# Expert lists ranked downwards by the first key, taken from the ninth block on, and built in bfloat16

## The chip, the cores and the metric

The program runs on one core of one Trainium2 chip. The metric is device time in microseconds of one execution. The five engines of the core are named as in the profile: PE (TensorE, with PEld for its weight loads), DVE (VectorE), ACT (ScalarE), POOL (GpSimd) and SP (which only issues transfers here). Each engine runs its instructions in the order of the program; semaphores make one wait for another.

## What is computed

Two transformer blocks over 256 tokens of width 2048. The change touches the first block's attention, its expert layer, and the second block's latent attention. The expert layer, cut from the reference:

```python
def peer(x, w_pq, sub_k1, sub_k2, u_emb, v_emb):      # 8 heads, 128 keys in each half, top 16
    q = (xt @ w_pq).reshape(T, PEER_HEADS, 2, PEER_HALF)
    s1 = jnp.einsum('thd,hkd->thk', q[:, :, 0], sub_k1, ...)
    s2 = jnp.einsum('thd,hkd->thk', q[:, :, 1], sub_k2, ...)
    v1, i1 = lax.top_k(s1, PEER_TOPK)
    v2, i2 = lax.top_k(s2, PEER_TOPK)
    cand = (v1[..., :, None] + v2[..., None, :]).reshape(T, PEER_HEADS, PEER_TOPK * PEER_TOPK)
    cidx = (i1[..., :, None] * N_KEYS + i2[..., None, :]).reshape(...)
    sc, sel = lax.top_k(cand, PEER_TOPK)
    eidx = jnp.take_along_axis(cidx, sel, axis=-1)
    gates = jax.nn.softmax(sc, axis=-1)
    ...
        act = jax.nn.gelu(jnp.einsum('cd,ced->ce', xc, u_emb[ic]))
        return jnp.einsum('ce,ced->cd', (gc * act).astype(...), v_emb[ic])
```

The first block's attention has 16 heads of width 64 in four groups that share a key head. The latent attention adds two products for a score: one over 128 columns of the head, and one over 64 rotary columns whose key is shared by all heads.

## The kernel before

**Arithmetic.** Every large product is a sum of three fp32r products of halves (`mm3`, lines 133 to 136): a weight tile `raw` of 128x2048 arrives by DMA, ACT rounds each half of it to `whi` (L123), DVE takes the rest as `wlo` (L124), and PE multiplies 12 times 512 columns for each half. `whi` and `wlo` have four buffers each, so DVE and ACT run at most four halves ahead of PE.

**The expert layer.** All 16384 rows of `u_emb` are multiplied (the u phase): 32 chunks of 512 experts, which is four values of key 1 each, in the order of key 1. A chunk is 8 halves, 8 transposes of the activations, and two DMAs into a table `AG` in DRAM, whose row is (key 1 + 1) x 128 + key 2. Beside it, DVE, ACT and a little of PE work out the routing at a lower priority: the top 16 (`top16`), the gate tables (`gsb`, which SP writes into `AG` in four pieces, with a maximum `um` over each, L679), and then the lists. A list says which experts are used: list A by both token tiles (42 blocks of 128 places), list B by the first tile alone (29), list C by the second alone (30). The order of an expert in its list is its rank, counted upwards in key 1 by a scan over `colsum` (L715).

**The lists.** Each of 16 steps (L742 to L753, J = 8) builds on DVE a one-hot `ln` of the lane (L744), a one-hot `b1` of the block (L746) and a product `bb` (L750); ACT builds the other half of `bb` (L749). PE then adds eight products of `ln` and `bb` into one PSUM bank (L753). `ids`, `idv` and `idg` (L755 to L763) are the finished lists. `ln`, `b1` and `bb` have two buffers each.

**The v phase.** For each block of a list, POOL gathers 128 rows of `v_emb` (`raw` or `vraw`, by `idv`) and the rows of `AG` for two or four blocks at once (`vag`, by `idg`). `gated` multiplies activation and gate into `vh` (L827), splits it into `vhh` and `vhl`, and PE adds 12 or 24 products into eight PSUM banks `acc`. POOL, DVE, ACT and PE take all this in the order in which a scheduler put it when the program was built; the schedule holds for all engines.

**Attention.** `attn1` (first block) makes the scores of two heads on partitions 0 to 63 of `qT` and `kT`, then of two on 64 to 127 (L444), and `softmax_out` multiplies the transposed weights `pT` with the values (L429): heads 0 and 1 into output partitions 0 to 63, heads 2 and 3 into 64 to 127. The latent attention (L1110, L1111) alternates a product over 128 partitions with one over 64. A fp32 matmul of the program is two MATMUL instructions in the trace.

Of the kernel before, what the change touches and what calls it, by code (L numbers as in the profile page):

```python
# [18 lines left out]
ALU = mybir.AluOpType  # L19
# [37 lines left out]
def tile_kernel(ctx: ExitStack, tc: tile.TileContext, A, out):  # L57
# [355 lines left out]
    def softmax_out(s, l, nh, vget, oget):  # L413
# [3 lines left out]
        for h in range(nh):  # L417
            V.tensor_scalar(s[:, h, :], s[:, h, :], r[:, h:h + 1], None, op0=ALU.mult)
        for h in range(0, nh, 2):
# [6 lines left out]
            S.activation(pT, tp.rearrange("p (a t) -> p a t", a=4), AF.Copy)  # L426
            for hh in range(2):
# [7 lines left out]
    def attn1(c, f, tt, qT):  # L435
# [4 lines left out]
        for e in range(2):  # L440
            ps = bank("sc")
            b = slice(e * 64, e * 64 + 64)
            for j in range(2):
                TE.matmul(ps[:, j * T:(j + 1) * T], lhsT=qT[b, 2 * f + j, tt * P:(tt + 1) * P],  # L444
                          rhs=kT[b, g, :], start=True, stop=True)
            V.tensor_tensor(s[:, 2 * e:2 * e + 2, :], ps.rearrange("p (a t) -> p a t", a=2),
                            maskb[:, tt, :].unsqueeze(1).to_broadcast([P, 2, T]), op=ALU.add)
# [6 lines left out]
        for h in range(4):  # L454
# [7 lines left out]
                    lambda h: ob[h // 2 * 64:h // 2 * 64 + 64, h % 2 * P:(h % 2 + 1) * P])  # L462
# [72 lines left out]
    nunc = xl_.tile([P, 1], I32, tag="nunc", name="nunc")  # L535
    u1 = ExitStack()
# [57 lines left out]
    for tt in range(2):  # L594
# [7 lines left out]
        sel = rt.tile([P, 8, 16], U32, tag="sel", name="sel")  # L602
        for h in range(8):
            cand = rt.tile([P, 16, 16], F32, tag="cand", name="cand", bufs=2)
            V.tensor_tensor(cand, v16[:, 2 * h, :].unsqueeze(2).to_broadcast([P, 16, 16]),
                            v16[:, 2 * h + 1, :].unsqueeze(1).to_broadcast([P, 16, 16]), op=ALU.add)
            top16(sc[:, h, :], sel[:, h, :], cand.rearrange("p a b -> p (a b)"), 256)
# [10 lines left out]
        for half, op, c in ((0, ALU.logical_shift_right, 4), (1, ALU.bitwise_and, 15)):  # L618
# [5 lines left out]
            for h in range(8):  # L624
                eq = rt.tile([P, 16, 16], F32, tag="eq", name="eq", bufs=2)
                V.tensor_tensor(eq, af[:, h, :].unsqueeze(2).to_broadcast([P, 16, 16]),
                                iota[:, 0:16].unsqueeze(1).to_broadcast([P, 16, 16]), op=ALU.is_equal)
                V.tensor_tensor(eq, eq, xf[:, 2 * h + half, :].unsqueeze(1).to_broadcast([P, 16, 16]),
                                op=ALU.mult)
                V.tensor_reduce(kf[:, h, :], eq, axis=AX.X, op=ALU.add)  # L630
# [21 lines left out]
    for c in range(4):  # L652
        gsb = gp.tile([P, P, 64], F32, tag="gsb", name="gsb", bufs=1)
        for t0 in range(0, 64, 4):
            t = 64 * c + t0
            io = iota.unsqueeze(1).to_broadcast([P, 4, P])
            oh = gp.tile([P, 4, P], F32R, tag="oh2", name="oh2", bufs=2)
# [3 lines left out]
            og = gp.tile([P, 4, 2, P], F32R, tag="og", name="og", bufs=2)  # L661
# [25 lines left out]

    kp = pool("places", 1, stack=r1p)
# [4 lines left out]
    iota1 = kp.tile([P, P], F32, tag="iota1", name="iota1")  # L693
# [24 lines left out]
    nA = kp.tile([P, 1], F32, tag="na", name="na")  # L718
    V.tensor_scalar(nA, tot[:, 0, P - 1:P], float(CAPA), None, op0=ALU.min)
    V.tensor_scalar(rk[:, 1, :], rk[:, 1, :], nA[:, 0:1], None, op0=ALU.add)  # L720
# [11 lines left out]
    lb = kt_("lb", 2)  # L732
# [548 lines left out]
```

## Time and profile before

| what | value |
|---|---|
| median of 3 runs (lowest, highest) | 3013.2 us (3012.96, 3013.81) |
| the profiled execution: time, span | 3017.87 us, 3016.0 us |
| mean granted clock of PE | 0.993 |
| PE busy | 2958.9 us, 98% |
| DVE busy | 2005.1 us, 66% |
| ACT busy | 1578.3 us, 52% |
| POOL busy | 270.7 us, 9% |
| HBM | 207 GB/s over the span |

Busy time of an engine is the time in which at least one of its instructions runs. PE is busy nearly throughout, so the time is its work and what little idle time it has; the granted clock says how much of full speed it had while it worked. A row of the timeline gives the start, the duration, the engine, the line, output and inputs, and in brackets the engine's idle time before it with what ended that.

### The profile page before, as it was taken

The numbers are of one execution on the slowest core, as the hardware profiler recorded it, in microseconds if no ns is written. First come the engines' busy times: TensorE is split into PE (matmuls) and PEld (weight loads), VectorE is DVE, ScalarE is ACT, GpSimd is POOL, SyncE is SP. The second block draws the span as 40 slices with busy tenths as digits, with TensorE's granted clock in tenths as the row PEclk, the third lists the DMA queues.
The fourth block names the chain that finished last, engine by engine and source line by source line (L and its number), as shares of the span: only waits on it lengthen the run. The fifth ranks groups of instructions, "written<-read, shape, count | busy, mean of one in ns | idle before, by whom it ended". The sixth has DMA issues, their size and how long they took to land. (4 is left out here: it accounts for less than half of the span.)

```text
span 3016.0 us, 36313 instructions
## 1 busy us (share of the span) xinstructions
PE 2958.9 (98%) x13729; PEld 2437.0 (81%) x13729; DVE 2005.1 (66%) x2958; ACT 1578.3 (52%) x2221; POOL 270.7 (9%) x232
## 2 busy tenths in 40 slices
PE   9999999999999999699999999999999999999999
PEld 7887888887888878588887788878888888888887
DVE  6886689977778769577777666754655445445454
ACT  6754545565666655455556455544444444344443
POOL 0000000000000000677661000000000000000000
PEclk9999999999999999899999999999999999999999
DMA  6452546657576673788885555545655555555554
GB/s 227 157 182 98 198 175 202 219 190 243 197 250 199 235 246 118 268 337 315 332 319 206 174 178 189 201 151 202 236 190 181 196 184 192 196 193 184 195 188 161
DMA packets 197296, 626.26 MB, mean 208 GB/s; under 512 B 82816, under 2 KB 116224, under 8 KB 129792
## 3 DMA queue, kind: packets, MB, share of 16 engines
q1 hardware_dynamic: 139520, 477.33, 46.0%
q0 software_dynamic: 20784, 124.79, 11.1%
q10 hardware_dynamic: 36816, 21.81, 2.4%
q8 instruction: 108, 1.77, 0.2%
q14 instruction: 68, 0.56, 0.1%
HBM read 583.77 MB, written 40.11 MB: 207 GB/s over the span
## 5 line engine op out<-in xcount | busy, mean ns | idle before, releaser
L124 DVE TENSOR_TENSOR wlo<-raw,whi 128x1024 fp32r<-128x1024 f32 (+1 forms) x844 | 1026.5, 1221 | 705.2 <-ACT whi L123 683.9
L123 ACT ACTIVATE whi<-raw 128x1024 fp32r<-128x1024 f32 (+1 forms) x844 | 889.6, 1058 | 960.3 <-PE lin L136 823.8
L135 PE MATMUL lin<-wlo,x1th 128*128 128x512 f32 x1152 | 453.0, 393 | 8.5 <-DVE wlo L124 8.5
L136 PE MATMUL lin<-whi,x1tl 128*128 128x512 f32 x1152 | 452.6, 393 | 0.0
L134 PE MATMUL lin<-whi,x1th 128*128 128x512 f32 x1152 | 445.7, 395 | 0.4 <-ACT whi L123 0.4
L136 PE MATMUL lin<-whi,x3tl 128*128 128x512 f32 x704 | 274.9, 391 | 0.0
L135 PE MATMUL lin<-wlo,x3th 128*128 128x512 f32 x704 | 274.2, 389 | 0.0
L134 PE MATMUL lin<-whi,x3th 128*128 128x512 f32 x704 | 269.6, 390 | 0.0
L135 PEld LDWEIGHTS lin<-wlo,x1th 128*128 128x128 f32 x1152 | 217.5, 189 | 52.1 <-DVE wlo L124 10.2
L136 PEld LDWEIGHTS lin<-whi,x1tl 128*128 128x128 f32 x1152 | 217.3, 189 | 42.4
L134 PEld LDWEIGHTS lin<-whi,x1th 128*128 128x128 f32 x1152 | 217.1, 189 | 41.7 <-ACT whi L123 0.8
L135 PE MATMUL lin<-wlo,y1th 128*128 128x512 f32 x512 | 201.6, 394 | 0.8 <-DVE wlo L124 0.8
L134 PE MATMUL lin<-whi,y1th 128*128 128x512 f32 x512 | 200.2, 397 | 1.7 <-ACT y1th L160 1.2
L136 PE MATMUL lin<-whi,y1tl 128*128 128x512 f32 x512 | 199.5, 395 | 0.8 <-DVE y1tl L161 0.8
L124 DVE TENSOR_TENSOR wlo<-uraw,whi 128x1024 fp32r<-128x1024 f32 x128 | 155.8, 1221 | 51.6 <-ACT whi L123 50.9
L123 ACT ACTIVATE whi<-uraw 128x1024 fp32r<-128x1024 f32 x128 | 135.2, 1058 | 103.7 <-PE lin L136 101.4
L135 PEld LDWEIGHTS lin<-wlo,x3th 128*128 128x128 f32 x704 | 132.2, 188 | 27.2
L136 PEld LDWEIGHTS lin<-whi,x3tl 128*128 128x128 f32 x704 | 132.2, 188 | 27.1
L134 PEld LDWEIGHTS lin<-whi,x3th 128*128 128x128 f32 x704 | 132.2, 188 | 27.0
L130 POOL DMA_INDIRECT raw<-in_v_dram,idv x61 | 80.2, 1315 | 684.9 <-DVE idg L763 637.6
L130 POOL DMA_INDIRECT vag<-ag,idg x102 | 134.0, 1313 | 53.1 <-issue 27.4
L136 PE MATMUL lin<-whi,at 128*128 128x512 f32 x352 | 137.2, 390 | 0.0
(442 smaller groups left out, 5046.3 us busy)
## 6 DMA issues: line engine op xcount, KB each, us to landing
raw<-in_w_in_dram SPq DMA_DIRECT2D x91, 1024.0 KB, 4.8
raw<-in_w_gu_dram SPq DMA_DIRECT2D x88, 1024.0 KB, 4.8
uraw<-in_u_dram SPq DMA_DIRECT2D x64, 1024.0 KB, 4.8
raw<-in_u_dram SPq DMA_DIRECT2D x64, 1024.0 KB, 4.9
raw<-in_w_dn_dram SPq DMA_DIRECT2D x44, 1024.0 KB, 4.8
raw<-in_w_out_dram SPq DMA_DIRECT2D x16, 1024.0 KB, 4.8
raw<-in_w_pq_dram SPq DMA_DIRECT2D x16, 1024.0 KB, 4.8
ag<-actT ACTq DMA_DIRECT2D x64, 256.0 KB, 3.0
```

The source lines that it names most:

```text
L123: S.activation(h[:, q], r, AF.Copy)
L124: V.tensor_sub(l[:, q], r, h[:, q].bitcast(F32))
L130: G.indirect_dma_start(out=dst, out_offset=None, in_=src, in_offset=bass.IndirectOffsetOnAxis(ap=rows, axis=0))
L134: TE.matmul(ps, lhsT=xh, rhs=wh, start=start, stop=False)
L135: TE.matmul(ps, lhsT=xh, rhs=wl, start=False, stop=False)
L136: TE.matmul(ps, lhsT=xl, rhs=wh, start=False, stop=stop)
```

## The change

Six things are done.

1. **Ranking.** The scan over `colsum` runs from the last key 1 to the first. List B begins at a fixed place behind list A's capacity instead of at list A's end. The blocks of each list are taken in the order 8, 9, ..., then 0 to 7 (`LATE`, `turn`). A value of key 1 has at most 128 experts, so a block from the ninth on holds no expert of the eight highest values of key 1, which are the last two chunks of the u phase; its gather reads `AGa`, the table without these rows.
2. **Early buffers.** The buffers of the v phase (`vag`, `vh`, `vhh`, `vhl`, `vraw`) come from a pool `ve` that is opened before the u phase's main loop. The first two blocks are multiplied together, bank by bank in the order 1, 2, 3, 0.
3. **Lists in bfloat16.** The iota, lane, block and `iota1` operands are bfloat16, and the layout is turned: `ln` is [128, J] and `b1` is [NL, J] with the step's eight columns innermost. DVE reads and writes neighbouring elements; each matmul reads its weights and its moving columns eight elements (16 bytes) apart.
4. **Routing.** The additions and comparisons of eight heads are one instruction of 2048 elements each instead of eight of 256. `oh2` and `og` get a third buffer.
5. **`attn1`.** The score matmuls alternate between the two halves of the partitions, and the value matmuls between the two halves of the output partitions (`pairs`).
6. **Latent attention.** The shared rotary key is written twice into `krz`, each time with the other 64 partitions zero, and L1111's product runs over 128 partitions. `krT` moves into the ring `hn`.

The diff, cut to its core:

```diff
+            if pairs and h == 0:
+                continue
             for hh in range(2):
                 for kk in range(2):
-                    TE.matmul(oget(h + hh), lhsT=vget(h + hh, kk), rhs=pT[:, 2 * hh + kk, :],
-                              start=kk == 0, stop=kk == 1)
+                    for i, pT in enumerate(pTs if pairs else pTs[-1:]):
+                        hd = 2 * i + hh if pairs else h + hh
+                        TE.matmul(oget(hd), lhsT=vget(hd, kk), rhs=pT[:, 2 * hh + kk, :],
+                                  start=kk == 0, stop=kk == 1)
...
+        pss = [bank("sc"), bank("sc")]
+        for j in range(2):
+            for e, ps in enumerate(pss):
+                b = slice(e * 64, e * 64 + 64)
                 TE.matmul(ps[:, j * T:(j + 1) * T], lhsT=qT[b, 2 * f + j, tt * P:(tt + 1) * P],
                           rhs=kT[b, g, :], start=True, stop=True)
...
+            eq = rt.tile([P, 8, 16, 16], F32, tag="cand", name="eq", bufs=1)
+            V.tensor_tensor(eq, af.unsqueeze(3).to_broadcast([P, 8, 16, 16]),
+                            iota[:, 0:16].unsqueeze(1).unsqueeze(1).to_broadcast([P, 8, 16, 16]), op=ALU.is_equal)
+            V.tensor_tensor(eq, eq, halfof(xf, half, 2), op=ALU.mult)
+            V.tensor_reduce(kf, eq, axis=AX.X, op=ALU.add)
...
-        V.tensor_tensor_scan(tot[:, i, :], tri[:, 1, :], cs[:, i, :], 0.0, op0=ALU.mult, op1=ALU.add)
+        V.tensor_tensor_scan(tot[:, i, ::-1], tri[:, 1, :], cs[:, i, ::-1], 0.0, op0=ALU.mult, op1=ALU.add)
...
-    lb = kt_("lb", 2)
+    lb = kt_("lb", 2, BF16)
...
+    iox = kp.tile([P, P, J], BF16, tag="iox", name="iox")
+    V.tensor_copy(iox, iota.unsqueeze(2).to_broadcast([P, P, J]))
...
-        ln = kp.tile([P, J, P], BF16, tag="ln", name="ln", bufs=2)
-        V.tensor_tensor(ln, iota.unsqueeze(1).to_broadcast([P, J, P]), bc(lane, j, P), op=ALU.is_equal)
+        ln = kp.tile([P, P, J], BF16, tag="ln", name="ln", bufs=2)
+        V.tensor_tensor(ln, iox, bc(lane, j, P), op=ALU.is_equal)
...
-                TE.matmul(ids2, lhsT=ln[:, i, :], rhs=bb[:, :, i, :], start=j + i == 0, stop=j + i == P - 1)
+                TE.matmul(ids2, lhsT=ln[:, :, i], rhs=bb[:, :, :, i], start=j + i == 0, stop=j + i == P - 1)
...
+    v0 = ExitStack()
+    ve = v0.enter_context(tc.tile_pool(name="vearly", bufs=1, side="right"))
...
+    LATE = 8
+    AGa, AG2a = AG[0:(P + 1 - LATE) * P, :], AG2[0:2 * (P + 1 - LATE) * P, :]
+    def turn(lo, n):
+        return [lo + (i + LATE) % n for i in range(n)]
...
-                gather(ag[:, i * 512:(i + 1) * 512], AG, idg[:, x:x + 1])
+                gather(ag[:, i * 512:(i + 1) * 512], AGa if b >= LATE else AG, idg[:, x:x + 1])
...
+    krz = mq.tile([P, 2, T], F32, tag="krz", name="krz")
+    G.memset(krz, 0.0)
+    for e in range(2):
+        b = slice(64 * e, 64 * e + 64)
+        V.tensor_copy(krz[b, e, :], krT[b, 0, :])
...
-                    TE.matmul(o, lhsT=qrT[b, h // 2, t], rhs=krT[b, 0, :], start=False, stop=True)
+                    TE.matmul(o, lhsT=qrT[:, h // 2, t], rhs=krz[:, e, :], start=False, stop=True)
```

**Where the lists end.** On DVE, from the last `wlo` of the u phase to the finished lists, in the kernel before (the buffer numbers of `b` and `bb` count the steps):

```order
L124 TENSOR_TENSOR wlo<-uraw,whi 128x1024 x2
L746 TENSOR_TENSOR b_5812<-iota,lb 128x808
L744 TENSOR_TENSOR ln<-iota,lb 128x1024
L750 TENSOR_TENSOR bb_5799<-b_5797,iota_5573 128x808
L744 TENSOR_TENSOR ln<-iota,lb 128x1024
L750 TENSOR_TENSOR bb_5814<-b_5812,iota_5573 128x808
L746 TENSOR_TENSOR b_5827<-iota,lb 128x808
L746 TENSOR_TENSOR b_5842<-iota,lb 128x808
L744 TENSOR_TENSOR ln<-iota,lb 128x1024
L750 TENSOR_TENSOR bb_5829<-b_5827,iota_5573 128x808
L744 TENSOR_TENSOR ln<-iota,lb 128x1024
L750 TENSOR_TENSOR bb_5844<-b_5842,iota_5573 128x808
```

The same engine behind the last `wlo` of the u phase in the changed kernel, first rows:

```order
L124 TENSOR_TENSOR wlo<-uraw,whi 128x1024
L758 TENSOR_TENSOR ln<-iox,lb 128x1024
L764 TENSOR_TENSOR bb_5631<-b_5629,iota_5435 128x808
L758 TENSOR_TENSOR ln<-iox,lb 128x1024
L764 TENSOR_TENSOR bb_5646<-b_5644,iota_5435 128x808
L760 TENSOR_TENSOR b_5659<-iox,lb 128x808
L760 TENSOR_TENSOR b_5674<-iox,lb 128x808
L758 TENSOR_TENSOR ln<-iox,lb 128x1024
L764 TENSOR_TENSOR bb_5661<-b_5659,iota_5435 128x808
```

Six steps instead of four stand behind the last `wlo`, and the steps begin 12 `wlo` ahead of the end instead of 18; in both kernels `idg` and all gathers come after them.

On PE, the end of the u phase in the kernel before (the last u matmul, the first list matmul behind it):

```order
L134 MATMUL lin<-whi,x1th 128x512
L135 MATMUL lin<-wlo,x1th 128x512
L136 MATMUL lin<-whi,x1tl 128x512
L753 LDWEIGHTS ln
L753 MATMUL x<-bb_5799,ln 128x202
```

and in the changed kernel:

```order
L134 MATMUL lin<-whi,x1th 128x512
L135 MATMUL lin<-wlo,x1th 128x512
L136 MATMUL lin<-whi,x1tl 128x512
L767 LDWEIGHTS ln
L767 MATMUL x<-bb_5661,ln 128x202
```

In both, four of the sixteen groups of eight list matmuls stand behind the last u matmul: two, then the eight transposes of the last chunk, then two more. Ahead of it the groups move: the first stands 10.8 halves before the end instead of 16.8.

On PE, the scores and values of the second half of `attn1` in the kernel before (here with buffer numbers, which tell the two banks and the two `pT` apart):

```order
L444 MATMUL sc_1948<-kT_1341,qT_1934 128x256 x2
L429 MATMUL ob_1744<-pT_1756,v_1340 64x128 x4
L429 MATMUL ob_1744<-pT_1767,v_1340 64x128 x4
L444 MATMUL sc_1952<-kT_1341,qT_1934 128x256 x2
L136 MATMUL lin_2422<-whi_2425,yll_826 128x512
```

and in the changed kernel:

```order
L452 MATMUL sc_1948<-kT_1341,qT_1934 128x256
L452 MATMUL sc_1949<-kT_1341,qT_1934 128x256
L436 MATMUL ob_1744<-pT_1756,v_1340 64x128
L436 MATMUL ob_1744<-pT_1763,v_1340 64x128
L436 MATMUL ob_1744<-pT_1756,v_1340 64x128
```

The matmuls of the two halves now follow each other in turn; in the rest of this half, runs of two score matmuls on one half of the partitions become runs of three or four over both.

## Rows read from the trace of the kernel before

**Rows 1.** The page, part 1: busy time, share of the span, instructions.
```profile
PE 2958.9 (98%) x13729; PEld 2437.0 (81%) x13729; DVE 2005.1 (66%) x2958; ACT 1578.3 (52%) x2221; POOL 270.7 (9%) x232
```

**Rows 2.** Waits of PE: line and releaser, us in total, times, longest.
```profile
PE tp L134 <- ACT vhh L829: 19.0, 1, 19.0
PE lin L135 <- DVE wlo L124: 11.1, 8, 2.8
```

**Rows 3.** Busy time by stretch (us, then engines, clock, DMA share, GB/s).
```profile
1147.00:1212.00 65.00, 65.00 (x362) 53.31 (x361) 60.65 (x61) 35.27 (x41) 0.00 (x0) 1.00 0.25 82
1212.00:1236.00 24.00, 3.14 (x26) 2.44 (x25) 8.67 (x15) 4.83 (x7) 13.15 (x13) 0.61 0.70 256
1236.00:1249.00 13.00, 10.44 (x29) 7.53 (x29) 7.62 (x9) 5.16 (x6) 10.26 (x10) 0.66 0.84 291
```

**Rows 4.** Timeline of PE from the u phase to the v phase.
```profile
1210.48 1.58 PE L753 MATMUL x<-bb,ln 128*128 128x202 bf16 x16
...
1235.55 0.79 PE L134 MATMUL tp<-whi,vhh 128*128 128x512 f32 x1 [19.03 <-ACT vhh L829]
1236.14 0.63 PE L135 MATMUL tp<-wlo,vhh 128*128 128x512 f32 x1
1236.57 0.63 PE L134 MATMUL sc<-whi,vhh 128*128 128x512 f32 x1
```

**Rows 5.** Timelines of DVE and POOL in the same stretch.
```profile
1218.07 0.21 DVE L763 CAST idg<-idf 128x101 uint32<-128x101 f32 x1
...
1234.08 0.69 DVE L827 TENSOR_TENSOR vh<-vag 128x512 f32<-128x512 f32 x1 [3.24 <-DMA vag<-ag,idg]
...
1218.63 1.09 POOL L130 DMA_INDIRECT raw<-in_v_dram,idv  x1 [637.58 <-DVE idg L763]
```

**Rows 6.** DVE groups by line and shape: busy us, mean ns, idle before.
```profile
L744 DVE TENSOR_TENSOR ln<-iota,lb 128x1024 bf16<-128x1024 f32 x16 | 19.5, 1220 | 4.4 <-PE x L753 4.2
L750 DVE TENSOR_TENSOR bb<-b,iota 128x808 bf16<-128x808 bf16 x16 | 15.9, 992 | 0.0
...
L704 DVE TENSOR_TENSOR m<-used,m 128x256 f32<-128x256 f32 x1 | 0.4, 427 | 0.0
...
L701 DVE TENSOR_SCALAR used<-used 128x256 f32<-128x256 f32 x1 | 0.3, 294 | 0.0
```

**Rows 7.** Timeline of PE: runs of score and of value matmuls in `attn1`.
```profile
184.68 1.14 PE L444 MATMUL sc<-kT,qT 64*128 64x256 f32 x8
...
203.50 1.58 PE L429 MATMUL ob<-pT,v 128*64 128x128 f32 x16
...
251.98 1.13 PE L444 MATMUL sc<-kT,qT 64*128 64x256 f32 x4
...
271.77 1.09 PE L429 MATMUL ob<-pT,v 128*64 128x128 f32 x8
```

**Rows 8.** PE groups by line and shape: busy us, mean ns, idle before.
```profile
L753 PE MATMUL x<-bb,ln 128*128 128x202 bf16 x128 | 13.8, 251 | 1.8 <-DVE bb L750 1.8
...
L1111 PE MATMUL sc<-krT,qrT 64*128 64x256 f32 x32 | 11.1, 428 | 0.0
L1110 PE MATMUL sc<-kT,qT 128*128 128x256 f32 x32 | 10.6, 412 | 0.0
L1018 PE MATMUL sc<-kT,qT 128*128 128x256 f32 x32 | 8.0, 379 | 0.0
```

**Rows 9.** ACT groups by line and shape, all reading PSUM.
```profile
L673 ACT ACTIVATE gh<-sc 128x256 f32<-128x256 f32 x128 | 46.3, 377 | 45.7 <-PE sc L668 45.4
...
L464 ACT ACTIVATE sqt<-ob 128x256 f32<-128x256 f32 x8 | 3.0, 380 | 12.2 <-PE ob L429 12.2
...
L489 ACT ACTIVATE qT<-tp 128x512 f32<-128x512 f32 x4 | 2.3, 596 | 2.2 <-PE tp L486 2.2
```

**Rows 10.** DVE and PE at the end of the first gate table.
```profile
697.69 8.86 DVE L679 TENSOR_REDUCE um<-gsb 128x32 f32<-128x2048 f32 x4
...
707.74 0.50 PE L135 MATMUL lin<-wlo,x1th 128*128 128x512 f32 x1 [2.73 <-DVE wlo L124]
```

More of the change, by code (lines that the diff above doesn't have):

```diff
@@ L535, in tile_kernel @@
     nunc = xl_.tile([P, 1], I32, tag="nunc", name="nunc")
+    fill2 = xl_.tile([P, 16], F32, tag="fill2", name="fill2")
+    G.memset(fill2, 0.0)
     u1 = ExitStack()
@@ L602, in tile_kernel, with halfof @@
         sel = rt.tile([P, 8, 16], U32, tag="sel", name="sel")
+        def halfof(x, half, axis):
+            x = x.rearrange("p (h s) a -> p h s a", s=2)[:, :, half, :]
+            return x.unsqueeze(axis).to_broadcast([P, 8, 16, 16])
+        cand = rt.tile([P, 8, 16, 16], F32, tag="cand", name="cand", bufs=1)
+        V.tensor_tensor(cand, halfof(v16, 0, 3), halfof(v16, 1, 2), op=ALU.add)
         for h in range(8):
[L604 to L607, printed above, removed]
+            top16(sc[:, h, :], sel[:, h, :], cand[:, h].rearrange("p a b -> p (a b)"), 256)
         g = rt.tile([P, 8, 16], F32, tag="gate", name="gate")
@@ L813, in tile_kernel @@
     VE = A["v"].rearrange("b p d -> (b p) d")
-    RA = list(range(NA))
-    RB = sorted(range(NA, NL), key=lambda b: (b - NA) % NB * 2 + (b >= NA + NB))
+    LATE = 8
+    AGa, AG2a = AG[0:(P + 1 - LATE) * P, :], AG2[0:2 * (P + 1 - LATE) * P, :]
+    def turn(lo, n):
+        return [lo + (i + LATE) % n for i in range(n)]
+    RA = turn(0, NA)
+    RB, RC = turn(NA, NB), turn(NA + NB, NC)
+    RB = [b for i in range(max(NB, NC)) for r in (RB, RC) for b in r[i:i + 1]]
     order = sorted([((i + 0.5) / (NA - 2), b) for i, b in enumerate(RA[:-2])] +
@@ L839, in prepare @@
             return
-        ag = vp.tile([P, 1024], F32, tag="vag", name="vag", bufs=3)
+        ag = ve.tile([P, 1024], F32, tag="vag", name="vag", bufs=3)
         if b < NA:
@@ L848, in prepare @@
         else:
-            end = NA + NB if b < NA + NB else NL
+            beg, end = (NA, NA + NB) if b < NA + NB else (NA + NB, NL)
             bs = list(range(b, min(b + 4, end)))
             for i, x in enumerate(bs):
-                gather(ag[:, i * 256:(i + 1) * 256], AG2, idg[:, x:x + 1])
+                gather(ag[:, i * 256:(i + 1) * 256], AG2a if b - beg >= LATE else AG2, idg[:, x:x + 1])
             hh, hl = gated(ag, len(bs))
@@ L855, in prepare @@
                 got[x] = [(hh[:, i], hl[:, i])] * 2
-    fresh = [True, True]
+    fresh = {(tt, c): True for tt in range(2) for c in range(4)}
     def vblock(b, vh, vl, cs, stop=False):
@@ L862, in vblock @@
                 hh, hl = got[b][tt]
-                mm3(acc[c][tt], hh, hl, vh[c], vl[c], fresh[tt], stop)
-        for tt in tiles_of(b):
-            fresh[tt] = False
-    last = []
+                mm3(acc[c][tt], hh, hl, vh[c], vl[c], fresh[tt, c], stop)
+                fresh[tt, c] = False
+    last, two = [], []
     for i, b in enumerate(order):
@@ L873, in tile_kernel @@
             break
-        raw = vp.tile([P, 2048], F32, tag="vraw", name="vraw", bufs=2) if i % 5 in (1, 3) else None
+        raw = ve.tile([P, 2048], F32, tag="vraw", name="vraw", bufs=2) if i % 5 in (1, 3) else None
         vh, vl = wtile(VE, rows=idv[:, b:b + 1], raw=raw)
-        vblock(b, vh, vl, range(4))
+        if i < 2:
+            two.append((b, vh, vl))
+            if i == 1:
+                for c in (1, 2, 3, 0):
+                    for w in two:
+                        vblock(*w, (c,))
+        else:
+            vblock(b, vh, vl, range(4))
     for b in order[-2:]:
@@ L929, in tile_kernel @@
     v1.close()
+    v0.close()
     lists.close()
```

47 lines of the change are left out of this document (18 added, 29 removed).

## The prediction

> **What bounds the kernel now.** I read the busy times first: PE is busy for 98% of the span [rows 1], so an instruction taken from PE is time won wherever PE does not then wait, and work of DVE and ACT counts only where PE waits for it. The waits of PE come next. One stands out: 19.0 us, once, for the first `vhh` of the v phase; the next largest are eight waits for `wlo` with 11.1 us together [rows 2]. The stretches around the large one show its size: from 1147 to 1212 us PE is busy without a gap, from 1212 to 1236 it works 3.14 of 24 us, and from 1236 to 1249 it works at a mean granted clock of 0.66 [rows 3], where 1 is the 2.4 GHz level and 0.5 the 1.2 GHz one. At the lower one matmuls start 0.43 us apart (1236.14, 1236.57) [rows 4]; in the full stretch 362 instructions take 65 us, 0.18 each with short ones among them [rows 3].
>
> The chain across the gap: the lists' last matmuls stand behind the last u matmul at 1210.48 [rows 4], `idg` is written at 1218.07, POOL issues the first gather at 1218.63, the first gathered `vag` gives `vh` at 1234.08 [rows 5], and PE starts at 1235.55 [rows 4]. From the first gather to PE's start are 16.9 us, which no step of the lists shortens. The question for this change is therefore when `idg` is written, as against the last u matmul.
>
> **The lists.** DVE worked 60.65 of 65 us in that stretch [rows 3]; a list step cost 1.22 us for `ln`, 0.99 for `b1` (same size as `bb`) and 0.99 for `bb` [rows 6], about 3.2 us, 16 times. With every operand in bfloat16 and neighbours innermost, the cost lies between this and half of it. The trace has no `tensor_tensor` of bfloat16 alone; the nearest row of a fast form is a `tensor_scalar` of 256 elements at 294 ns beside a `tensor_tensor` of 256 at 427 [rows 6], which is half the time per element once a fixed part of 160 ns is taken off (267 ns against 134). I take half: 0.69 + 2 x 0.58 = 1.85 us a step, 16 x 1.35 = 21.6 us less DVE work. That by itself is off the path.
>
> What counts is the order. The steps now begin 12 `wlo` before the end of the u phase instead of 18, and six steps instead of four come behind the last `wlo`. One `wlo` is worth 12 matmuls, which at half of the 0.43 us of the lower level are 2.6 us of PE, so the start is 16 us later and the saving is 22 us. Four of sixteen groups of list matmuls stand behind the last u matmul as before, and the chain through them is the same: two groups, the transposes (which wait for ACT's `act`), two halves of `bb` on ACT, two groups, and the small steps from `ids` to `idg`. The DVE part of this chain, two `ln` and two `bb`, shrinks from 4.4 to 2.5 us, and ACT's halves of `bb`, which stay as they are, take over as the last to come. I expect `idg` some 7 us after the last u matmul instead of 7.8 (1210.48 to 1218.28 [rows 4, 5]): **-0.8 us** (from -2 to +2). So the gathers do not move into the last chunks of the u phase, whatever table they read, and the 19 us wait stays. `AGa` frees the first gathers from the last two chunks' writes, but these were not what they waited for: POOL waited for `idg` [rows 5].
>
> **The list matmuls.** They were 128 matmuls at 13.8 us busy [rows 8]; sixteen take 1.58 us with the tail of the last [rows 4], so about 0.09 us each, 0.42 ns for each of 202 columns. They now read both operands 16 bytes apart. The trace has no PE read at such a distance. The nearest rows are ACT's: `gh` reads PSUM with neighbours 1 KB apart and takes 377 ns for 256 elements, while `sqt` reads 256 neighbours in 380 [rows 9]. So distance costs ACT nothing, but ACT takes (596 - 380) / 256 = 0.84 ns per element [rows 9], half PE's pace. What is proven is a distant read at 0.84 ns, which would make a matmul 0.17 us: +0.08 x 128 = +11 us, all on PE in a stretch in which PE has no gap [rows 3]. The lower end is 0. I take **+10 us**, near the proven pace, and keep 0 as a rival. The Trainium skill, page "SBUF — State Buffer", section "Door 1: The DMA port swizzle", speaks against this edit: memory lines are 16 bytes, full bandwidth needs two hits on a line, and each step to a new line pays. By it, at one read for two PE cycles, the term would be 128 x 0.084 = +10.8 us (an estimate from that page), which is about the sum I make from ACT's rows; no run here shows it yet.
>
> **`attn1`.** Eight instructions (four score matmuls, two on each half) take 1.14 us in a row, and four (two on one half) 1.13 [rows 7]: the halves of the array already work beside each other where the four stand together. The first half of `attn1` had that; in the second, runs of two and singles become runs of three or four. Before: seven runs of two and two singles; after: three runs of up to four and three singles; 4 x 1.13 - 0.6 (a single, estimated at half a run) is 3.9 us less. The values: sixteen instructions, eight on one output half and then eight on the other, take 1.58 us, and eight take 1.09 [rows 7]. In turn the sixteen should cost what eight do. Six runs of sixteen and one split into two of eight are seen as such; over eight calls this is 7 x 0.49 + 1.09 = 4.5 us. Together 8.4 us; the end of `attn1` has short waits of PE for ACT and DVE which would eat a part: **-7 us** (-4 to -8.5). If the halves did not overlap for values, 3.5 would be left.
>
> **Latent attention.** L1110 and L1111 in turn are busy 10.6 + 11.1 us for 64 instructions; 32 of the same 256 columns over 128 partitions alone (L1018) 8.0 [rows 8]. With `krz` all 64 are of that kind: 21.7 - 16.0 = 5.7; the tails in busy time overlap, so **-5 us** (-4 to -6). The two copies on DVE and a memset on POOL lie long before and cost nothing; were their cover gone, 0.5 us each.
>
> **The rest.** The routing's instructions over eight heads save DVE the fixed part of 98 instructions (112 become 14), about 15 us, in a stretch where PE waits for nothing. Four times in the u phase, however, four `um` reduces of 8.86 us together hold DVE, and PE waits up to 2.73 us for the `wlo` behind them [rows 10]; they stay, in slightly other places among the `wlo`: **-1.5 us** (-4 to +2). A third buffer for `oh2` and `og` bears on nothing that PE waits for. The ranking and the order of the blocks change no count: 101 blocks with the same products.
>
> **The sum** goes against the profiled execution: span 3016.0 and 1.9 us around it, which lies 4.7 us above the median of the runs. -0.8 + 10 - 7 - 5 - 1.5 = -4.3, so 3013.6 for it and **3009 us** for the median. Faster or slower by 0.2% (6 us) is about what a measurement of this kernel can tell from no change.
>
> **The rivals.**
> *The distant reads cost nothing* (0.30). For it: ACT's row; against it: PE reads at twice ACT's pace. Without the +10: 2999 us, faster. Here L753's successor stays near 13.8 us busy.
> *The weight loads no longer hide* (0.11), the slower side. If the 128 columns of weights are read at the same 0.84 ns, 0.11 us, and not beside the 202 of the matmul before them, a list matmul costs 0.28 us: +0.19 x 128 = 24 us in place of 10, 3013 - 14 + 24 = 3023 us. It decides from the point at which load and columns share one read path. For it: both operands are distant now; against it: a load ran beside the matmul so far.
> *bfloat16 gives DVE nothing* (0.05). Then 16 steps at 3.2 us begin 16 us later: six steps behind the last `wlo` are 19 us instead of 11, and the ten before them cost DVE 13 us more than PE's pace leaves it, of which I estimate 5 to show, so `idg` comes about 13 us later: 3022 us, slower.
> *The change does what it says* (0.04): `idg` comes before the last two chunks, the gathers hide, the wait of 19 us goes, and with it some 5 us of the lower clock: 3009 - 24 = 2985 us. Against it stands the order of DVE, in which `idg` follows the last `wlo`.
>
> **How the numbers follow.** The forecast, with its bounds from 3004 to 3015, has 0.48; about a third of it lies below 3007. Faster: 0.30 + 0.04 + 0.14 = 0.48. Slower: 0.11 + 0.05 and a little for stalls of the new order, 0.17. Within 0.2%: 0.35. The likeliest case's own range is 3004 to 3015. The range of eight in ten runs from 2995, the lower bound of the first rival less the spread of the u phase, to 3023.
>
> **What would show it.** In the changed profile: L767 (the list matmuls) busy about 24 us is the forecast, 14 the first rival, 38 the second; `ln` at 0.69 us; PE's wait for the first `vhh` still 17 to 20 us with `idg` behind the last u matmul; runs of sixteen value instructions at 1.1 us; L1147 and L1148 (the latent scores) at 16 us together. Wrong would be: `idg` before the last u matmul, or new waits of PE for `wlo` between steps of the lists.

## The result, and the profile after

The changed kernel takes 3053.6 us (median of 4 runs, 3052.8 to 3056.2), the kernel before beside it 3013.4: a ratio of 1.0135, 95% interval 1.0117 to 1.0153. It is 40 us slower; the forecast was 3009 and the range ended at 3023. The profiled execution has a span of 3053.7 us.

PE waits for the same things as before, and for no longer. Waits of PE in the changed kernel (line and releaser, us in total, times, longest):

```profile
PE sc L134 <- ACT vhh L853: 18.7, 1, 18.7
PE lin L135 <- DVE wlo L124: 7.3, 8, 1.7
...
PE sc L134 <- ACT whi L123: 4.9, 1, 4.9
```

The 19 us for the first `vhh` stay ([rows 2]: 19.0), the eight waits for `wlo` fell from 11.1 to 7.3. So the loss is not idle time but work of PE. Groups of the changed kernel (busy us, mean ns, idle before); the first answers to L753 in [rows 8], with 13.8 us:

```profile
L767 PE MATMUL x<-bb,ln 128*128 128x202 bf16 x128 | 48.0, 544 | 0.0
L767 PEld LDWEIGHTS <-ln 128*128 128x128 bf16 x128 | 18.1, 147 | 26.0 <-issue 25.6 <-DVE wlo L124 0.3
L758 DVE TENSOR_TENSOR ln<-iox,lb 128x1024 bf16<-128x1024 bf16 x16 | 11.1, 692 | 37.8 <-PE x L767 37.8
L764 DVE TENSOR_TENSOR bb<-b,iota 128x808 bf16<-128x808 bf16 x16 | 9.1, 572 | 0.0
L760 DVE TENSOR_TENSOR b<-iox,lb 128x808 bf16<-128x808 bf16 x16 | 8.7, 572 | 0.0
```

The list matmuls cost 34 us more, with not a gap before them. DVE does its steps in half the time and then stands still 37.8 us because PE has not yet read the `ln` of two steps ago. The timeline of PE in the changed kernel, at the end of the u phase (compare [rows 4]):

```profile
1233.89 0.63 PE L135 MATMUL lin<-wlo,x1th 128*128 128x512 f32 x1
1234.32 0.63 PE L136 MATMUL lin<-whi,x1tl 128*128 128x512 f32 x1
...
1237.94 0.40 PE L136 MATMUL lin<-whi,x1tl 128*128 128x512 f32 x1
1238.18 6.00 PE L767 MATMUL x<-bb,ln 128*128 128x202 bf16 x16
1244.00 1.89 PE L809 MATMUL tp<-ident,act 128*128 128x128 f32 x8
1245.68 5.98 PE L767 MATMUL x<-bb,ln 128*128 128x202 bf16 x16
1270.42 0.80 PE L134 MATMUL sc<-whi,vhh 128*128 128x512 f32 x1 [18.75 <-ACT vhh L853]
```

Sixteen list matmuls take 6.00 us where they took 1.58 [rows 4], and two such runs stand between the last u matmul and the lists' end. The u matmuls of 1234 us start 0.43 us apart, which is the lower level of the clock, although PE had no gap there. The stretches show it (columns as in [rows 3]; the granted clock, here a mean over 25 us, is the third number from the end):

```profile
1150.00:1175.00 25.00, 25.00 (x94) 17.76 (x93) 16.51 (x30) 11.11 (x12) 0.00 (x0) 0.86 0.32 105
1175.00:1200.00 25.00, 25.00 (x78) 15.51 (x77) 9.13 (x14) 8.49 (x11) 0.00 (x0) 0.73 0.05 15
1200.00:1225.00 25.00, 25.00 (x82) 15.48 (x81) 11.59 (x16) 7.75 (x8) 0.00 (x0) 0.86 0.02 7
1225.00:1250.00 25.00, 25.00 (x77) 13.85 (x76) 5.71 (x10) 6.46 (x8) 0.00 (x0) 0.69 0.07 21
```

Before, PE was as full from 1147 to 1212 us at a clock of 1.00 [rows 3]. Later, in the v phase, fewer matmuls fit into the same time. Fifty microseconds of the kernel before, and then of the changed kernel:

```profile
1410.00:1460.00 50.00, 50.00 (x222) 41.42 (x221) 36.67 (x36) 28.89 (x31) 34.90 (x28) 1.00 0.88 326
```

```profile
1410.00:1460.00 50.00, 50.00 (x217) 40.54 (x216) 36.10 (x36) 28.47 (x30) 33.31 (x26) 1.00 0.91 340
```

PE is busy throughout and at full clock in both, but it does 217 matmuls in place of 222: 0.2304 us each in place of 0.2252. The v phase has 1716 of them by the groups of the trace, so this is about 9 us, which nothing that the diff does to the arithmetic explains.

### The profile page after: what moved, and what is told of

Read it like the earlier page. It is cut to its first block, busy times and chain, and to the rows that moved or that the text cites. A ratio compares the mean times of both kernels' runs of the same rounds, so it can differ in the third digit from the quotient of the medians.

```text
span 3053.7 us, 36236 instructions
## 1 busy us (share of the span) xinstructions
PE 2997.5 (98%) x13729; PEld 2450.4 (80%) x13729; DVE 1976.3 (65%) x2860; ACT 1580.4 (52%) x2220; POOL 271.4 (9%) x233
## 3 DMA queue, kind: packets, MB, share of 16 engines
q0 software_dynamic: 20736, 124.66, 11.1%
q8 instruction: 108, 1.77, 0.2%
## 5 line engine op out<-in xcount | busy, mean ns | idle before, releaser
L135 PE MATMUL lin<-wlo,x1th 128*128 128x512 f32 x1152 | 456.3, 396 | 4.8 <-DVE wlo L124 4.8
L136 PE MATMUL lin<-whi,x1tl 128*128 128x512 f32 x1152 | 456.6, 396 | 0.0
L134 PE MATMUL lin<-whi,x1th 128*128 128x512 f32 x1152 | 450.2, 398 | 1.8 <-ACT whi L123 1.8
```

The lines of the kernel that those rows point to most:

```text
L134: TE.matmul(ps, lhsT=xh, rhs=wh, start=start, stop=False)
L135: TE.matmul(ps, lhsT=xh, rhs=wl, start=False, stop=False)
L136: TE.matmul(ps, lhsT=xl, rhs=wh, start=False, stop=stop)
```

## The experiments

Theory A: the list matmuls' operands 16 bytes apart make the loss. Theory B: the new order of the work does. When neither was enough, others were added: E (the batched selection of part 4), F (parts 1 and 2 as a whole), G (the buffers of part 2) against H (the order and the other table of part 1), and I (the byte address of the buffers) against J (the region or the early pool). Ratios are to the kernel before on the same chip.

### Which operand, and how far apart (runs 1 to 4 and 15)

Run 1 undoes part 3 alone:

```diff
-        ln = kp.tile([P, P, J], BF16, tag="ln", name="ln", bufs=2)
-        V.tensor_tensor(ln, iox, bc(lane, j, P), op=ALU.is_equal)
+        ln = kp.tile([P, J, P], BF16, tag="ln", name="ln", bufs=2)
+        V.tensor_tensor(ln, iota.unsqueeze(1).to_broadcast([P, J, P]), bc(lane, j, P), op=ALU.is_equal)
...
-                TE.matmul(ids2, lhsT=ln[:, :, i], rhs=bb[:, :, :, i], start=j + i == 0, stop=j + i == P - 1)
+                TE.matmul(ids2, lhsT=ln[:, i, :], rhs=bb[:, :, i, :], start=j + i == 0, stop=j + i == P - 1)
```

> The changed kernel with the lists' two operands laid out and typed as before (each matmul's elements side by side, equality in float32); the rest of the change stays. Theory A (the list matmuls' reads 16 bytes apart are what the 40 us are made of): 128 list matmuls back at 13 to 14 us of busy time and 0.08 to 0.09 us each in a run of eight, u matmuls in the stretch of 1150 to 1250 us at the clock of before (0.90 and above), and the time at before less what attn1 (15.2 to 11.4 and 13.2 to 9.2 us) and the latent scores (21.7 to 19.0 us) save in the trace of after: 3013 - 10 = 3003, 2998 to 3008. Theory B (the new order, the ranking upwards or the values gathered early lose it): 3030 or more, with the list matmuls at 14 us all the same.

Measured: ratio 1.0016 (1.0006 to 1.0025), 3020.7 us. Part 3 costs 0.0119, or 36 us, so A holds for the bulk; but 3003 was expected, and 17 us are still missing. The list matmuls are busy 17.3 us where 13 to 14 were expected: the last five groups of eight ran at the lower level of the clock. In run 1, the matmuls and what PE waits for in them:

```profile
L765 PE MATMUL x<-bb,ln 128*128 128x202 bf16 x128 | 17.3, 288 | 8.1 <-DVE bb L762 8.1
```

The other two parts of the 36 us: the three u products are busy 445.1 + 452.3 + 452.3 us in run 1 and 450.2 + 456.3 + 456.6 in after, 13.4 us more. The clock of run 1 from 1150 to 1200 us:

```profile
1150.00:1175.00 25.00, 25.00 (x134) 20.44 (x134) 24.93 (x32) 14.88 (x17) 0.00 (x0) 1.00 0.32 106
1175.00:1200.00 25.00, 25.00 (x149) 20.71 (x147) 22.65 (x23) 13.20 (x16) 0.00 (x0) 1.00 0.07 22
```

List matmuls 48.0 - 17.3 = 30.7, u matmuls 13.4, less the 8.1 us of waits that run 1 has and after has not: 36 us, against 35.0 between the two spans. The records of matmuls that follow each other overlap, so busy times are a little too large; from start to start the u matmuls took 11.3 us more.

Runs 2 and 3 put one operand apart and leave the other together: run 2 reads `lhsT=ln[:, :, i], rhs=bb[:, :, i, :]`, run 3 `lhsT=ln[:, i, :], rhs=bb[:, :, :, i]`, each with its tile laid out to match.

> The changed kernel with only the stationary operand (ln) read 16 bytes apart; the 202 moving elements lie side by side again. In after one list matmul took 0.363 us: a load of 0.146 and columns of 0.22 one after the other. Theory A in series (each distant operand adds its own part, the load is not hidden): 0.146 + 0.085 = 0.23 us each, 30 us for 128 and a time of 3003 + 128 x 0.145 = 3021, up to 3028 with a lower clock. Theory A hidden (the load hides behind columns once these are quick): 0.15 us each, 3011. Theory C (the weights alone make the whole loss): 0.36 us each, 3050. Theory D (the columns alone): 0.09 us, 3003. Theory B: 3030 or more whatever the matmuls take.

> The changed kernel with only the 202 moving elements (bb) read 16 bytes apart; the 128 stationary ones lie side by side. Theory A (each distant operand adds its own part): columns 0.22 us, the load of before (0.1 us) hidden behind them, so 0.22 to 0.24 us each, 28 to 31 us for 128, time 3003 + 128 x 0.14 = 3021, up to 3028 with a lower clock. Theory C (weights alone): 0.09 us, 3003. Theory D (columns alone): 0.36 us, 3050. Theory B: 3030 or more whatever the matmuls take.

Measured: weights apart 1.0001 (0.9990 to 1.0011), 3015.7 us; columns apart 1.0130 (1.0113 to 1.0147), 3054.0 us, as slow as after. Theory D holds: the columns make all of it. Its time for run 2, 3003, was 13 us too low; that is what is missing in run 1 too, and the later runs explain it. Of run 2, from the timelines of PE and PEld:

```profile
1162.56 1.63 PE L771 MATMUL x<-bb,ln 128*128 128x202 bf16 x16
...
1180.04 0.93 PE L771 MATMUL x<-bb,ln 128*128 128x202 bf16 x8
...
1162.56 1.45 PEld L771 LDWEIGHTS <-ln 128*128 128x128 bf16 x16 [0.26 <-issue]
```

Eight more matmuls take 0.70 us, 0.0875 each, the pace of before (1.58 and 0.88); sixteen loads with distant weights pass in 1.45 us beside them. Each load's own record is longer (148 ns on average, 97 before), and that costs nothing. Of run 3:

```profile
1174.03 5.88 PE L771 MATMUL x<-bb,ln 128*128 128x202 bf16 x16
1187.29 3.02 PE L771 MATMUL x<-bb,ln 128*128 128x202 bf16 x8
```

Here eight more take 2.86 us: 0.36 each, 1.77 ns for each of 202 columns in place of 0.43. I had read after's trace as load and columns in a row (0.146 + 0.22); runs 2 and 3 say no: with the weights together it is 0.36 as well.

Runs 4 and 15 change one number, `J = 4` and `J = 16`: both operands are 8 and 32 bytes apart.

> The changed kernel with the lists worked out four values at a time in place of eight, so both operands are read 8 bytes apart instead of 16; twice as many steps on VectorE and ScalarE, of half the size. Theory A with a price in proportion to the distance: between 0.085 and 0.363 us, about 0.2 us each, 26 us for 128 and 3003 + 128 x 0.12 = 3018. Theory A with a step at some distance: either 0.36 us and 3050 as in after, or 0.09 us and 3003 to 3008. Theory B (the order loses it): no change from after, 3045 to 3060, or more by the added steps.

> The changed kernel with the lists worked out sixteen values at a time, so both operands are read 32 bytes apart. In the fourth run (8 bytes) the 128 list matmuls were busy 27.1 us, in after (16 bytes) 48.0, in the kernel before 13.8. A price in proportion to the distance would give 80 to 90 us and a time of 3085 or more; a price that is full from 16 bytes on (each element fetched alone) gives 46 to 50 us and 3045 to 3060.

Measured: 8 bytes 1.0030 (1.0019 to 1.0041), 3024.0 us; 32 bytes 3039.0 us in a single execution. First two rows of run 4, then one of run 15:

```profile
1179.37 0.90 PE L767 MATMUL x<-bb,ln 128*128 128x202 bf16 x4
...
1172.63 1.63 PE L767 MATMUL x<-bb,ln 128*128 128x202 bf16 x8
```

```profile
1181.15 12.08 PE L767 MATMUL x<-bb,ln 128*128 128x202 bf16 x32
```

Neighbours cost 0.0875 us, 8 bytes 0.18, 16 bytes 0.36: twice, and four times. At 32 bytes it is no more: 12.08 / 32 = 0.38, where the same division at 16 bytes gives 6.00 / 16 = 0.38. At 8 bytes the clock stays at 1.00 from 1150 to 1200 us, at 32 bytes it falls as in after (0.82 and 0.77). The price of distance itself does not follow the clock. The first run of sixteen in after begins at 1161.79 us at a granted clock of 1.00 and ends at 0.50 (from 1166 us on), and its matmuls start 0.36 us apart throughout; those of run 1, side by side, start 0.0875 us apart at the upper level and 0.168 at the lower one. So the 34 us are not the lower clock in another guise. Run 15 is faster than after although its matmuls cost the same (48.3 us): its lists were done ahead of the end of the u phase, and its wait for `vhh` is 3.6 us. Why they were done so early was not followed further.

### The selection (runs 5 to 7)

In run 1, `used` was ready at 1108.4 us, 7 us later than before, although the routing had begun 6 us earlier. Run 5 is run 1 with the selection by head again (8 x 256 elements instead of 2048 for `cand` and `eq`); run 6 adds `ln` in bfloat16 with its weights apart, as in run 2; run 7 adds that `tri` and `pidx` are loaded ahead of the routing:

```diff
+    trib = rp.tile([P, 2, P], BF16, tag="trib", name="trib")
+    pidx = rp.tile([P, 1], F32, tag="pidx", name="pidx")
+    nc.sync.dma_start(pidx, A["pidx"])
...
+    tri = rq.tile([P, 2, P], F32, tag="tri", name="tri")
+    nc.sync.dma_start(tri, A["tri"])
+    V.tensor_copy(trib, tri)
```

> The lists laid out as before (as in the first experiment) and the routing's selection by head as before: 112 instructions of 256 elements instead of 14 of 2048. In the first experiment the scores of the routing were done 5.8 us earlier than before, but the first gates came 3.2 us later and `used` 7 us later (1108.4 against 1101.5), and PE stood empty 8.1 us between the last list groups. Theory E (the batched selection makes the lists late, and the lists set the end of the u phase): `used` at 1096 to 1098, `idg` at about 1212, the wait for the lists back at 2 us, and the time at 3013.4 - 5.8 - 2.7 = 3005 (3001 to 3008). Theory F (early buffers, ranking upwards or gathers of the other table cost the time): 3017 to 3021 as in the first experiment.

> As the run before, and `ln` in bfloat16 with its weights read 16 bytes apart (columns together). It takes 16 x 0.53 = 8.5 us from VectorE in the lists; between the first two experiments that moved `idg` by 6.2 us (1218.3 to 1212.1). Theory E: where VectorE's list steps set the end, `idg` comes up to 6 us earlier than in the run before and the time is 2999 to 3005; where PE's last u matmuls do, the two runs are equal. Theory F: 3013 to 3016.

> As the run before, and the ranking's two constants (`tri`, `pidx`) loaded before the routing instead of behind the last writes of the gates. Before, `used` was ready at 1101.5 and the first step that needs the constant ran at 1132.9. Theory E: the lists begin some 20 us earlier, `idg` is written ahead of the last u matmul, the first gathers run beside the last chunks, and of the 19 us wait of PE half or more goes: 2985 to 2995. If the gathers or the v phase's first products cannot begin earlier for another reason (a buffer, a queue), the wait stays at 17 to 20 us although `idg` is early, and the time is 2999 to 3005.

Measured: 1.0000 (0.9990 to 1.0010), 3013.8 us; 0.9981 (0.9971 to 0.9990), 3009.4 us; 0.9947 (0.9931 to 0.9964), 2998.2 us. Each lies 3 to 6 us above the range expected of it. Run 5 stands between theory E (3001 to 3008) and F (3017 to 3021): `used` and `idg` came as early as E says or earlier, but the step from run 1 is 5 to 7 us instead of 16. The 10 us that the place of the buffers costs, shown below, are in all three runs, and with them E's times come out. The steps from run 5 to 6 and to 7 are as E has them. `used` and `idg` in run 1, then in run 5:

```profile
L714 DVE TENSOR_SCALAR used<-used x1: 284/284/284, 1108.4 to 1108.4; 128x256 f32<-128x256 f32 x1
...
L775 DVE CAST idg<-idf x1: 216/216/216, 1218.3 to 1218.3; 128x101 uint32<-128x101 f32 x1
```

```profile
L713 DVE TENSOR_SCALAR used<-used x1: 293/293/293, 1093.2 to 1093.2; 128x256 f32<-128x256 f32 x1
...
L774 DVE CAST idg<-idf x1: 215/215/215, 1208.2 to 1208.2; 128x101 uint32<-128x101 f32 x1
```

The batched selection has 12 us less to do on DVE (for `eq` alone, twelve instructions of 2.28 us against 96 of 0.41) and yet hands on 15 us later. The rows of `cand` show where most of that begins, in run 1 and then in run 5:

```profile
L619 DVE TENSOR_TENSOR cand<-v x2: 2269/2274/2279, 440.4 to 525.3; 128x2048 f32<-128x2048 f32 x2
```

```profile
L616 DVE TENSOR_TENSOR cand<-v x16: 401/408/418, 363.6 to 523.0; 128x256 f32<-128x256 f32 x16
```

The sum over all eight heads cannot start before the last head's scores are there, at 440.4 us; by head, it starts at 363.6. From 360 to 440 us DVE worked 66.3 us in run 5 and 53.6 in run 1, and from 440 to 520 it was full in both. So the gates (the last copy of `gT`) come 8 us later in run 1, 582.3 against 573.9. The other 7 us are lost in the gate tables behind it, which was not taken apart. The batched selection costs 0.0016, or 5 us, little more than the intervals allow. Run 6 is 6 us faster than run 5: bfloat16 pays on DVE for `ln`, as long as PE reads its columns side by side. For `bb`, whose layout then makes one operand the same value along the innermost axis, it pays nothing: 993 ns in run 6, as before, against 572 in after. Run 7 shows that the change's own aim can be had; the wait of PE for the first `vhh` in it:

```profile
PE sc L134 <- ACT vhh L856: 2.5, 1, 2.5
```

`idg` is written at 1190.2 us, before the last u matmul (1203), and 19 us of waiting have become 2.5.

### The rest of the attention's gain (runs 8 to 14)

Run 8 is the kernel before with parts 5 and 6 alone (the diff's pieces for `attn1` and `krz`).

> The kernel before with only the two edits of the attention (`attn1` in turn over the halves, the latent scores over 128 partitions). In the trace of after these rows fell by 3.8, 4.0 and 2.7 us. If both gains come through: 3013.4 - 10.5 = 3003 (3001 to 3007). If the gain of `attn1` is lost where the lists set the end of the u phase: only the latent scores' part is left, 3010 to 3012.

Measured: 0.9958 (0.9944 to 0.9972), 3003.2 us, as the first case had it. The score and value matmuls of `attn1` in the kernel before, and then with the latent scores in run 8:

```profile
L444 PE MATMUL sc<-kT,qT 64*128 64x256 f32 x64 | 15.2, 405 | 0.0
...
L429 PE MATMUL ob<-pT,v 128*64 128x128 f32 x128 | 13.2, 279 | 0.0
```

```profile
L452 PE MATMUL sc<-kT,qT 64*128 64x256 f32 x64 | 11.4, 408 | 0.0
L1124 PE MATMUL sc<-kT,qT 128*128 128x256 f32 x32 | 9.5, 379 | 0.0
L1125 PE MATMUL sc<-krz,qrT 128*128 128x256 f32 x32 | 9.5, 379 | 0.0
L436 PE MATMUL ob<-pT,v 128*64 128x128 f32 x128 | 9.2, 279 | 0.0
```

So parts 1 and 2, which run 5 has on top of run 8 (with the third buffers of part 4), cost 0.0042, 13 us. Runs 9 and 10 add one of them each to run 8: run 9 the pool `ve` without the new order, run 10 ranking, `turn` and `AGa` without the pool. Run 11 takes run 7 and puts three tiles back into `vp`:

```diff
-        h = ve.tile([P, 4, P], F32, tag="vh", name="vh", bufs=1)[:, 0:n]
+        h = vp.tile([P, 4, P], F32, tag="vh", name="vh", bufs=1)[:, 0:n]
-        hh = ve.tile([P, 4, P], F32R, tag="vhh", name="vhh", bufs=4)[:, 0:n]
+        hh = vp.tile([P, 4, P], F32R, tag="vhh", name="vhh", bufs=4)[:, 0:n]
-        hl = ve.tile([P, 4, P], F32R, tag="vhl", name="vhl", bufs=4)[:, 0:n]
+        hl = vp.tile([P, 4, P], F32R, tag="vhl", name="vhl", bufs=4)[:, 0:n]
```

> The kernel before with the two attention edits (as in the eighth run, 3003 us) and the v phase's buffers in a pool that is opened ahead of the u phase (`ve`), nothing else. In the runs with the whole of parts 1 and 2, 216 or 217 matmuls of the v phase fit into 50 us in place of 222, and the time from `idg` to the end was 1800 to 1803 us; in the eighth run it was 222 and 1791.6. Theory G (where the buffers lie, or that they are open early, slows the v phase's matmuls): 217 in 50 us here too, 3011 to 3014. Theory H (the order of the blocks, or the gathers of the other table): 222, 3001 to 3005.

> The kernel before with the two attention edits and part 1 alone: ranking downwards, list B at a fixed place, blocks taken from the ninth on, gathers from `AGa`; the v phase's buffers where they were. Theory H: 217 matmuls in 50 us of the v phase and 3011 to 3014. Theory G: 222, and 3001 to 3005.

> The seventh run's kernel (2998 us) with `vh`, `vhh` and `vhl` back in the v phase's own pool; `vag` and `vraw` stay in the early one, so the gathers still begin before the u phase ends. Theory G by the place of the stationary operands: 222 matmuls in 50 us and about 9 us off, 2988 to 2991; if the later opening of the pool delays the first `vhh`, a few us of that are lost again. Theory G by `vag` and `vraw`, or theory H: 217 and 2996 to 3001.

Measured: 0.9965 (0.9951 to 0.9979), 0.9966 (0.9954 to 0.9979) and 0.9921 (0.9905 to 0.9938). Neither half makes the 13 us; run 10 has 222 matmuls in 50 us, so H falls. Run 9 has 220, where G expected 217, and run 11 again 222:

```profile
1410.00:1460.00 50.00, 50.00 (x220) 41.05 (x219) 37.17 (x36) 29.36 (x32) 36.17 (x28) 1.00 0.87 322
```

```profile
1410.00:1460.00 50.00, 50.00 (x222) 41.40 (x221) 35.48 (x36) 28.65 (x31) 30.50 (x22) 1.00 0.84 305
```

These tiles lie 64 bytes apart in run 9 and in after (220 and 217), which suggested the address itself. (The 64 bytes are `fill2`, an unused tile that the change also adds.) Run 12 is the changed kernel, and run 13 run 7, with `vh`, `vhh` and `vhl` (and `vag`) 128 bytes lower:

```diff
-        raw = ve.tile([P, 2048], F32, tag="vraw", name="vraw", bufs=2) if i % 5 in (1, 3) else None
+        raw = ve.tile([P, 2064], F32, tag="vraw", name="vraw", bufs=2)[:, 0:2048] if i % 5 in (1, 3) else None
```

Run 14 goes the other way: run 8 with a tile of 128 bytes ahead of `vag`.

> The changed kernel with one thing different: the two `vraw` buffers are 64 bytes longer each, so `vag`, `vh`, `vhh` and `vhl` lie 128 bytes lower in each partition (`vhh` from byte 186496 instead of 186624; in the kernel before it was 181376). Modulo 512 bytes `vhh` then lies at 128, as in the kernel before and in the eleventh run (169088), where 222 matmuls of the v phase fit into 50 us; at 256 (after) it were 217, at 320 (the ninth run) 220. Theory I (the remainder of the address sets the pace of the v phase's matmuls): 222 and 9 us less than after, 3045 (3042 to 3048). Theory J (it is the region above some byte, or the early pool itself): 217 to 220 and 3050 to 3056.

> The seventh run's kernel with the same 128 bytes. Theory I: 222 in 50 us and 9 us less than in the seventh run, a ratio of 0.9917 to the kernel before instead of 0.9947 (2988 to 2990), and better than the eleventh, where PE waited 5.2 us for the first `vhh`. Theory J: 0.994 to 0.995.

> The eighth run's kernel (attention edits only, buffers of the v phase in their own pool as before) with a tile of 128 bytes ahead of `vag`, so `vhh` lies at byte 181504, at 256 modulo 512. Theory I: 217 in 50 us and 9 us more than the eighth run, a ratio of about 0.999 (3010 to 3014). Theory J: 222 and a ratio of 0.995 to 0.9965.

Measured: 1.0110 (1.0093 to 1.0127), 3047.1 us, against 1.0135; 0.9911 (0.9895 to 0.9928), 2989.3 us, against 0.9947; 0.9992 (0.9982 to 1.0001), 3011.3 us, against 0.9958. Fifty microseconds of runs 12, 13 and 14 in turn:

```profile
1410.00:1460.00 50.00, 50.00 (x222) 41.41 (x221) 37.43 (x37) 29.77 (x32) 33.82 (x27) 1.00 0.90 337
```

```profile
1410.00:1460.00 50.00, 50.00 (x222) 41.41 (x222) 35.58 (x36) 29.45 (x32) 30.79 (x23) 1.00 0.84 303
```

```profile
1410.00:1460.00 50.00, 50.00 (x217) 40.56 (x216) 36.62 (x36) 29.11 (x31) 34.54 (x28) 1.00 0.87 319
```

Theory I holds, both ways. The first `vhh` lies at byte 181376, 169088 and 186496 of a partition where 222 fit, at 186688 where 220 do, and at 186624 and 181504 where 217 do. The remainder by 256 is 128 in the first three, 64 in the fourth, 0 in the last two (by 512 it is 128, 320 and 256; the runs do not tell the two apart). `vag` and `vraw` are not what counts: in run 11 both lie at a remainder of 0 by 256, and the pace is 222. The weight loads' records do not grow with it: 188 to 191 ns on average before, 188 to 192 in after. Of the 13 us of parts 1 and 2, the place is about 10 (run 14 less run 8); the 2 to 3 that are left are no more than the intervals allow (run 10: 0.9966 against 0.9958).

Run 13 is 0.9% faster than the kernel before and the best of all: parts 1, 2, 5 and 6, the third buffers of part 4, a gain by bfloat16 in `ln` alone, the selection by head, the constants early, and the buffers 128 bytes lower.

## Why the prediction was wrong

The ladder from before to after, each step the difference of two measured ratios, in us of 3014 (each good to some 4 to 6 us by the intervals):

| step | ratio | us |
|---|---|---|
| parts 5 and 6 (run 8) | 0.9958 | -12.7 |
| parts 1 and 2, third buffers (run 5) | 1.0000 | +12.7 |
| batched selection (run 1) | 1.0016 | +4.8 |
| lists in bfloat16, turned (after) | 1.0135 | +35.9 |

**The step that failed is the term of the list matmuls.** I put it at +10 us and let +11 be its end, because ACT reads distant elements at 0.84 ns [rows 9] and I took that for the proven pace of any engine. It measured +34 us of busy time, and part 3 as a whole +36: PE pays 1.77 ns for each distant column, worse than ACT. A row of another engine was no bound, and those rows read PSUM, while PE reads its columns from SBUF. The estimate from the Trainium skill (page "SBUF — State Buffer", section "Door 1: The DMA port swizzle"), +10.8 us, was too small by about the same factor. Its 16-byte line agrees with the runs in that 32 bytes cost no more than 16. Its two hits on a line do not suffice here: at 8 bytes apart each line is hit twice, and the matmul took 0.18 us instead of 0.0875.

**The clock was not in the sum at all.** I took the price of a matmul and not what it does to its neighbours: the u matmuls among the distant ones took 11 us more than in run 1 (13.4 by busy time), in stretches at 0.69 to 0.86 of full clock. The term should have been two, and the second alone is as large as the whole of what I had put down.

**The second rival had the sign and not the mechanism.** It gave 3023 us by weight loads that no longer hide. Run 2 shows that they hide as before, and run 3 that the columns do it alone. The first rival, that distance costs nothing, is true of the weights.

**Early buffers had no price.** I wrote that the ranking and the order of the blocks change no count, which is so; the new place of the tiles has no term in the sum at all, which is a cost of nothing without a reason. Runs 12 to 14 put the place at 8 to 11 us. This could not have been read from the trace of before, but it could have been left open as a term: the tiles that the 1716 matmuls of the v phase load were moved.

**The routing cost nothing only while its cover lasted.** I said that PE waits for nothing there; what waits are the lists, at the other end of 500 us. Run 5 against run 1 makes that 5 us. In after itself this was not separated, since there the list matmuls set the pace.

**Right were** `ln` at 0.69 us and `b1` and `bb` at 0.58 (692 and 572 ns); the wait for the first `vhh` between 17 and 20 us (18.7), with `idg` behind the last u matmul; and the attention: -12 us forecast, -12.7 measured in run 8. The split held as well: `attn1` gained 3.8 + 4.0 us (7 forecast), the latent scores some 5 (5 forecast). Their two lines stay at 9.5 us each, but the records of the two overlap, and the sum counts that twice. In the kernel before, and then in run 8:

```profile
1988.88 0.70 PE L1111 MATMUL sc<-krT,qrT 64*128 64x256 f32 x2
1989.51 0.70 PE L1110 MATMUL sc<-kT,qT 128*128 128x256 f32 x2
1990.13 0.70 PE L1111 MATMUL sc<-krT,qrT 64*128 64x256 f32 x2
```

```profile
1981.41 0.59 PE L1125 MATMUL sc<-krz,qrT 128*128 128x256 f32 x2
1981.84 0.59 PE L1124 MATMUL sc<-kT,qT 128*128 128x256 f32 x2
1982.27 0.59 PE L1125 MATMUL sc<-krz,qrT 128*128 128x256 f32 x2
```

Two of them start every 0.43 us instead of 0.63. Counted once, all 64 are busy 15.4 us instead of 20.2, which is the 16 us of the prediction. The end of the lists, -0.8 us, failed with the matmuls: `idg` is written 15 us after the last u matmul (1253.2 against 1238.2) instead of 7, of which the two runs of sixteen are 12. The waits for `wlo` went down by 3.8 us where 1.5 was forecast, but with the batched selection: run 5, without it, has 11.1 us of them again.

The rival in which the change does what it says had the right reason against it. The gathers had to wait for `idg`, and `idg` for the lists; run 7 needed the constants early for the lists to be done in time.

**Open:** whether `vhh` or `vhl` is the tile whose place counts (they moved together, with `vh`, which PE does not read), by what mechanism, and whether the place itself or its relation to that of `whi` and `wlo` does: these begin at a remainder of 128 by 256 in all of these kernels, which is where the pace of 222 was seen. Open too is why the clock falls among the distant matmuls, and where the second half of the selection's delay comes from.

## What to carry to other kernels

Turning a layout to make one engine read neighbours moves the distance to the next reader: price it there, by a row of that engine, or measure it with one matmul before the rest is built on it. Here, at 16 bytes, it is free for the stationary operand and costs four times the columns for the moving one. When a pool moves, count the matmuls in a fixed stretch of a later phase that the diff does not touch: here a change of 2% at full clock and with no idle time led to where the tiles lie. Do not add the busy times of instructions that overlap; read their starts. A chain that is off PE's path for 500 us may still set when a phase can end; look for its last step, not for its first wait.

## What the runs showed of the hardware

- A bfloat16 matmul of 202 moving columns took 0.0875 us with the columns side by side, 0.18 at 8 bytes apart, 0.36 at 16 and no more at 32 (runs 2, 4, 3 and 15). With the 128 stationary columns 16 bytes apart it stayed at 0.0875, and the loads at one in 0.09 us (run 2).
- At 16 bytes the 0.36 us were the same at a granted clock of 1.00 and of 0.50 (after), while side by side it was 0.0875 us at the upper level and 0.168 at the lower one (run 1).
- While matmuls of 0.36 us stood among fp32r ones on a PE without a gap, the granted clock over 25 us fell to 0.69 to 0.86 (after); with 0.18 us each it stayed at 1.00 (run 4).
- An fp32r matmul of 512 columns starts every 0.2252, 0.2273 or 0.2304 us (222, 220, 217 in 50 us) as the tiles `vh`, `vhh` and `vhl` lay at a remainder of 128, 64 and 0 by 256 bytes; the last two are its stationary operands.
- A `tensor_tensor` on DVE with all operands in bfloat16 and neighbours innermost took 692 ns for 1024 elements, against 1220 with float32 inputs (after, before). With one bfloat16 operand the same value along the innermost axis, 808 elements took 993 ns, against 572 (run 6, after).
